# Sixteen modulation pieces moved into the filter loop, a re-staged Hyena loop, and a first token tile read partly from SBUF

## The chip, the cores and the metric

The kernel runs on one core of one Trainium2 chip. The metric is the device time of one execution in microseconds (us), as the median of several runs. Five engines work side by side: TensorE (PE in the rows; PEld is its weight load), VectorE (DVE), ScalarE (ACT), GpSimd (POOL), and SyncE (SP), which here issues nearly all DMAs. Engines wait for one another by semaphores, and each works through its own instructions in order.

## The reference

A two-layer diffusion backbone on 1024 latent tokens of width 1024, with 256 context tokens. What matters here is the first half of layer 0:

```
m  = silu(c) @ w_mod[l] + b_mod[l]              # six chunks of 1024: shift, scale, gate, twice
h  = rmsnorm(x) * (1 + scale) + shift
proj = h @ w_in                                  # 1024 x 2560: gate | RG-LRU input | Hyena (3 x 512)
y_a  = gelu(gate) * (RG-LRU forward + backward)  # 512 channels
u    = conv of 3 taps over the Hyena columns;  v, gate_0, gate_1 = split(u)
kf   = rfft of implicit filters (a small sine MLP times a decay window)
z = v
for o in (0, 1):
    z = gate_o * (irfft(rfft(z) * kf[o]) + bias * z)
x  = x + g1 * (concat(y_a, z) @ w_out)           # then expert-choice MoE; layer 1 follows
```

## The kernel before

All arithmetic is float32; the large products split each operand into a high and a low part and do three matmuls (`mm3`, L154 to L158), the split being one ACT copy and one DVE subtraction (`split`, L160 to L162). A framework turns this Python into one instruction list per engine: it ranks instructions by the order in which the program text issues them, and places each on its engine as soon as its own estimate says that operands and a buffer are free. So a later instruction of the text may run ahead of an earlier one that isn't ready, but once placed, an engine's order is fixed. Buffers with one tag rotate through a fixed count (`bufs`).

The stretches that the change touches, in order of time:

- **Modulation pieces.** `w_mod` is cut into pieces of 128 rows and 2048 columns, 1 MB each: 24 for layer 0, 16 (later 8 more) for layer 1. `ada_load` (L220) fetches one into a buffer of the pool `wr`, which has 4 buffers of 8 KB per partition; `ada_mm` (L227) multiplies it into one PSUM tile that collects 8 pieces (L235); `ada_end` (L253) closes a set of 8 with a copy, transposes and a store. `fill(n)` (L248) does one product and one load, n times. The first 8 pieces are worked off at the head of the filter loop, and the other 32 in the Hyena loop.
- **Filter loop** (`filters`, L397). Eight jobs, one for each 128 channels and each of the two orders. A job computes filter values (`signal`: products L413, windowed by DVE L414), transforms them on PE (L436 to L446), combines the results on DVE (L458 to L474) into a 1 MB tile K of the pool `wr`, and stores K to DRAM (`kd`, L475). Between the jobs, steps of the first norm run (transposes L326). PSUM has two pools: "n", 4 buffers of one bank, and "w", 2 buffers of two banks.
- **RG-LRU part**, not touched; then the **Hyena loop**. A `short(ct)` (L782) projects 128 channels (48 matmuls, L156 to L158), and applies the 3-tap conv with one ACT and two DVE instructions (L786 to L788). `tok` transposes a 128 x 1024 tile to token order on PE and copies it with ACT. A job J is one block of 128 channels at one order, and has five steps: `hy_fwd` (32 matmuls L612, and an ACT copy of half of each result, L615; it also fetches K), `hy_st1` (first butterfly, 8 DVE instructions with one operand in PSUM, L622 and L623), `hy_mid` (DVE only: an 8-point transform, the product with K, the way back; tiles raw/pq/E of tag "X", 3 buffers), `hy_inv` (16 matmuls on PE, L651) and `hy_gate` (two DVE products of the PSUM result and the gate, with stride, L659). Each of four rounds runs the job of order 0, then the job of order 1 on its result; `pend` and `drain` put a job's inverse and gate one step later.
- **Tail.** Two RG-LRU gates (`gate`, L737: projection, gelu, product with the scan's result L743, store to DRAM `ycd`), then, in an order written out by hand for PE, DVE and ACT (the `manual_schedule` block, L845 to L865), the splits of `w_out` (L986, L991), the last `drain`, a load of the first token tile's seven rows of blocks from `ycd` (`y_load`, L933), its split, and the first product of the output projection (`post_mm`). The `posts` of the other tiles follow, then the MoE.

## Time and profile before

| | us |
|---|---|
| median of 3 runs (lowest 2285.1, highest 2289.81) | 2288.9 |
| the profiled execution | 2288.93 |
| its span, from the first to the last instruction | 2287.0 |
| filter loop, from its first K to the first projection of the RG-LRU part | 31 to 128 |
| RG-LRU part | 128 to 267 |
| Hyena loop and tail, to the first matmul of the output projection | 267 to 552.4 |

Over the whole span PE is busy 93%, DVE 80%, ACT 53%. Such a share is an average over stages; the table by stretch shows where PE and DVE are both near full. A matmul's modelled time overlaps its neighbour's, so its price here is the distance from start to start.

### The profile page before, as it was taken

How to read it: one execution, taken by the hardware profiler on the slowest of the kernel's cores; microseconds unless marked ns; L12 is line 12 of the kernel's file. 1: busy time of each engine (PE TensorE's matmuls, PEld its weight loads, DVE VectorE, ACT ScalarE, POOL GpSimd, SP SyncE). 2: the span in 40 equal slices, each digit the busy share in tenths (PEclk: the TensorE clock that was granted, in tenths of full speed). 3: DMA queues.
4: the chain of work that ended last, by engine and by line, in shares of the span. 5: the costliest groups of instructions: out<-in, count | busy, mean ns of one | idle time of the engine just before them, and what ended most of it. 6: DMA issues, size and time to landing. Idle time of an engine off the chain costs nothing. (4 is left out here: it accounts for less than half of the span.)

```text
span 2287.0 us, 28692 instructions
## 1 busy us (share of the span) xinstructions
PE 2122.7 (93%) x10626; PEld 1653.2 (72%) x10626; DVE 1819.6 (80%) x2877; ACT 1201.4 (53%) x1458; POOL 126.8 (6%) x128
## 2 busy tenths in 40 slices
PE   7999998988967999999999899979679999999997
PEld 5976766756745877878778588867457777777775
DVE  5879799997596989999888534276968898888887
ACT  3658621213214777777777521134247777676774
POOL 0000000000001000000000100010010000000001
PEclk9999998989988999999999899989889999999999
DMA  7241573654848999999998744334679999999974
GB/s 283 102 138 47 194 274 122 228 195 150 293 171 313 367 395 375 391 385 377 393 377 307 233 129 154 104 119 180 254 293 365 389 367 388 370 376 379 372 268 156
DMA packets 210021, 616.09 MB, mean 269 GB/s; under 512 B 27988, under 2 KB 76758, under 8 KB 200089
## 3 DMA queue, kind: packets, MB, share of 16 engines
q1 hardware_dynamic: 198610, 572.84, 66.3%
q0 software_dynamic: 11248, 41.42, 7.1%
q8 instruction: 83, 1.36, 0.2%
q14 instruction: 56, 0.46, 0.1%
q10 hardware_dynamic: 24, 0.01, 0.0%
HBM read 558.62 MB, written 55.61 MB: 269 GB/s over the span
## 5 line engine op out<-in xcount | busy, mean ns | idle before, releaser
L162 DVE TENSOR_TENSOR e<-wx,e 128x1024 fp32r<-128x1024 f32 x516 | 617.6, 1221 | 87.0 <-ACT e L161 74.0
L161 ACT CAST e<-wx 128x1024 fp32r<-128x1024 f32 x516 | 540.2, 1051 | 226.1 <-PE P L158 224.0
L156 PE MATMUL P<-e,th 128*128 128x512 f32 x1384 | 562.9, 407 | 0.0
L158 PE MATMUL P<-e,tl 128*128 128x512 f32 x1384 | 543.5, 393 | 0.8 <-DVE tl L162 0.8
L157 PE MATMUL P<-e,th 128*128 128x512 f32 x1384 | 543.2, 392 | 0.0
L157 PEld LDWEIGHTS P<-e,th 128*128 128x128 f32 x1384 | 260.3, 188 | 60.9 <-DVE e L162 3.8
L156 PEld LDWEIGHTS P<-e,th 128*128 128x128 f32 x1384 | 260.1, 188 | 60.8 <-issue 7.2
L158 PEld LDWEIGHTS P<-e,tl 128*128 128x128 f32 x1384 | 259.9, 188 | 60.0 <-DVE tl L162 1.2
L162 DVE TENSOR_TENSOR e<-w,e 128x1024 fp32r<-128x1024 f32 x176 | 211.6, 1222 | 49.6 <-ACT e L161 29.4
L156 PE MATMUL P<-hh,wh 128*128 128x512 f32 x576 | 229.8, 400 | 16.4 <-DVE y L788 12.9
L161 ACT CAST e<-w 128x1024 fp32r<-128x1024 f32 x176 | 183.9, 1051 | 93.4 <-PE P L158 74.5
L157 PE MATMUL P<-hl,wh 128*128 128x512 f32 x576 | 229.3, 398 | 0.0
L158 PE MATMUL P<-hh,wlo 128*128 128x512 f32 x576 | 228.3, 397 | 0.1
L156 PEld LDWEIGHTS P<-hh,wh 128*128 128x128 f32 x576 | 109.5, 190 | 50.2 <-issue 24.0
L157 PEld LDWEIGHTS P<-hl,wh 128*128 128x128 f32 x576 | 109.5, 190 | 26.6 <-issue 4.3
L158 PEld LDWEIGHTS P<-hh,wlo 128*128 128x128 f32 x576 | 109.1, 189 | 26.4 <-issue 4.0
L1314 POOL DMA_INDIRECT acc<-yo,ix x31 | 50.7, 1635 | 923.9 <-DVE yo L1313 923.9
L162 DVE TENSOR_TENSOR tl<-q,th 128x512 fp32r<-128x512 f32 x128 | 84.7, 683 | 5.3 <-ACT th L161 4.1
L161 ACT CAST wh<-w 128x1024 fp32r<-128x1024 f32 x16 | 16.7, 1049 | 124.1 <-PE P L157 110.4
L1274 PE MATMUL P<-wx,xf 128*128 128x512 f32 x176 | 79.1, 592 | 0.0
L161 ACT CAST th<-q 128x512 fp32r<-128x512 f32 x128 | 71.8, 587 | 1.7 <-PE q L1239 1.7
L297 POOL TENSOR_TENSOR rs<-ms,nh 128x1 f32<-128x1 f32 x42 | 23.9, 570 | 830.2 <-issue 436.2
(411 smaller groups left out, 3022.8 us busy)
## 6 DMA issues: line engine op xcount, KB each, us to landing
wx<-i_exp_w SPq DMA_DIRECT2D x272, 1024.0 KB, 8.2
w<-i_exp_w SPq DMA_DIRECT2D x96, 1024.0 KB, 7.7
w<-i_w_mod SPq DMA_DIRECT2D x40, 1024.0 KB, 7.8
wst<-i_w_in SPq DMA_DIRECT2D x20, 512.0 KB, 4.5
kd<-w SPq DMA_DIRECT2D x8, 1024.0 KB, 5.2
w<-kd SPq DMA_DIRECT2D x8, 1024.0 KB, 8.5
acc<-res SPq DMA_DIRECT2D x16, 512.0 KB, 3.0
e<-i_exp_w SPq DMA_DIRECT2D x16, 512.0 KB, 8.0
```

The source lines that it names most:

```text
L156: t.matmul(o, lh, rh, start=start, stop=False)
L157: t.matmul(o, lh, rl, start=False, stop=False)
L158: t.matmul(o, ll, rh, start=False, stop=stop)
L161: self.nc.scalar.copy(hi, src)
L162: self.nc.vector.tensor_sub(lo, src, hi.bitcast(F32))
L297: nc.gpsimd.tensor_tensor(r, m, self.nh[:, :n], op=OP.pow)
L1274: nc.tensor.matmul(P[:, ns], f[:, k], h[:, ns], start=k == 0, stop=k == 7)
L1314: self.last = nc.gpsimd.indirect_dma_start(self.acc[l][:, :], bass.IndirectOffsetOnAxis(ap=xT[e][1][:, 0:1], axis=0), yo, None, compute_op ...
```

## The change

Three parts. In `filters`, each job but the first now does two `fill(1)` (and in jobs 1 and 2 one load more), and what is loaded is multiplied after the loop: 16 pieces that were multiplied in the Hyena loop. The Hyena loop is written anew: `hy_st1` is gone; `hy_fwd` lets ACT copy each result whole into an SBUF tile `raw`, and `hy_mid` does the first butterfly from it with two DVE instructions of 1024 columns and fetches K itself; after the inverse, ACT copies the result to SBUF (`hy_copy`), and the gate is one DVE product from SBUF; the job of order 1 now runs one round behind the job of order 0. Sixteen pieces are left in the loop: one load ahead and three `fill` in each round. Last, the first token tile takes the two blocks of the RG-LRU gates of the tail from their SBUF tiles, and the other five from `ycd` by two loads.

```diff
@@ -425,10 +425,15 @@
             if n:
                 for _ in range(3):
                     next(other, None)
+                self.fill(1)
+                if n < 3:
+                    self.ada_load()
             K = self.wr.tile([128, 8, 2, 128], F32, name="w", tag="w")
             q0 = self.ps.tile([128, 2, 2, 128], F32, name="q0", tag="n")
             qa = self.ps.tile([128, 4, 2, 128], F32, name="qa", tag="w")
             qb = self.ps.tile([128, 4, 2, 128], F32, name="qb", tag="w")
+            if n:
+                self.fill(1)
             for i in range(2):
                 mc = slice(i * 128, i * 128 + 128)
                 oc = slice(128 - i * 128, 256 - i * 128)
@@ -602,30 +607,23 @@
 
     def hy_fwd(self, p, J):
         nc = self.nc
-        J["K"] = K = self.wr.tile([128, 8, 2, 128], F32, name="w", tag="w")
-        nc.sync.dma_start(K, self.kd[J["o"]][J["qd"]])
-        J["q"] = []
+        J["raw"] = raw = p.tile([128, 8, 2, 128], F32, name="raw", tag="X", bufs=3)
         for a in range(4):
             q = self.ps.tile([128, 2, 2, 128], F32, name="q", tag="n")
             for j in range(2):
                 for ri in range(2):
                     nc.tensor.matmul(q[:, j, ri], self.G[:, a + 4 * j, ri * 128:ri * 128 + 128], J["u"][:, a + 4 * j],
                                      start=True, stop=True)
-            y4 = p.tile([128, 2, 128], F32, name="y4", tag="y4", bufs=2)
-            nc.scalar.copy(y4, q[:, 1])
-            J["q"].append((q, y4))
-
-    def hy_st1(self, p, J):
-        V = self.nc.vector
-        J["pq"] = pq = p.tile([128, 8, 2, 128], F32, name="pq", tag="X", bufs=3)
-        for a, (q, y4) in enumerate(J["q"]):
-            V.tensor_tensor(pq[:, a], q[:, 0], y4, op=OP.add)
-            V.tensor_tensor(pq[:, 4 + a], q[:, 0], y4, op=OP.subtract)
+            nc.scalar.copy(raw[:, a:a + 5:4], q)
 
     def hy_mid(self, p, J):
         V = self.nc.vector
-        pq, K = J["pq"], J["K"]
-        E = p.tile([128, 8, 2, 128], F32, name="E", tag="X", bufs=3)
+        K = self.wr.tile([128, 8, 2, 128], F32, name="w", tag="w")
+        self.nc.sync.dma_start(K, self.kd[J["o"]][J["qd"]])
+        E = J["raw"]
+        pq = p.tile([128, 8, 2, 128], F32, name="pq", tag="X", bufs=3)
+        V.tensor_tensor(pq[:, 0:4], E[:, 0:4], E[:, 4:8], op=OP.add)
+        V.tensor_tensor(pq[:, 4:8], E[:, 0:4], E[:, 4:8], op=OP.subtract)
         sub = p.tile([128, 4, 2, 128], F32, name="sub", tag="sub", bufs=1)
         self.fft8(pq, E, -1, sub)
         Z = pq
@@ -651,13 +649,15 @@
                     self.nc.tensor.matmul(q[:, j], J["Z"][:, a, ri], self.IG[:, a, ri], start=ri == 0, stop=ri == 1)
             J["r"].append(q)
 
-    def hy_gate(self, p, J):
-        dst = p.tile([128, D], F32, name="zt", tag="zt", bufs=1)
-        zv = dst.rearrange("q (p a) -> q a p", a=8)
-        gv = J["gate"].rearrange("q (p a) -> q a p", a=8)
+    def hy_copy(self, p, J):
+        J["z"] = p.tile([128, D], F32, name="zt", tag="zt", bufs=2)
+        zv = J["z"].rearrange("q (p a) -> q a p", a=8)
         for h, q in enumerate(J["r"]):
-            self.nc.vector.tensor_tensor(zv[:, h * 4:h * 4 + 4], q, gv[:, h * 4:h * 4 + 4], op=OP.mult)
-        return dst
+            self.nc.scalar.copy(zv[:, h * 4:h * 4 + 4], q)
+
+    def hy_gate(self, J):
+        self.nc.vector.tensor_tensor(J["z"], J["z"], J["gate"], op=OP.mult)
+        return J["z"]
 
     def to_tok(self, src, dst):
         nc = self.nc
@@ -707,6 +707,8 @@
                         yield from self.norm_steps(pn, rows[i], self.gg[0][0], self.mod[0], hh[i], hl[i], dve=False, hb=2)
 
                 self.filters(fk, halves())
+                while self.ada_have:
+                    self.ada_mm()
             wl = pool(sl, "wl")
             src = A["w_in"].rearrange("(k p) n -> p k n", p=128)
 
@@ -742,6 +744,7 @@
                 nc.scalar.activation(ge, P, AF.Gelu_apprx_tanh, bias=0.0, scale=1.0)
                 nc.vector.tensor_tensor(ge, ge, hs, op=OP.mult)
                 nc.sync.dma_start(self.ycd[ct * 128:(ct + 1) * 128, :], ge)
+                return ge
 
             with ExitStack() as s2:
                 pcx = pool(s2, "pcx")
@@ -789,50 +792,47 @@
                 return y
 
             def tok(y):
-                ut = py.tile([128, 8, 128], F32, name="ut", tag="u", bufs=2)
+                ut = py.tile([128, 8, 128], F32, name="ut", tag="u", bufs=1)
                 self.to_tok(y, ut)
                 return ut
 
-            pend = []
-
-            def drain():
-                J = pend.pop(0)
+            def inverse(J):
                 self.hy_inv(py, J)
-                z = self.hy_gate(py, J)
-                if J["o"] == 0:
-                    return tok(z)
-                i = J["qd"]
-                if i == 3:
-                    return z
-                nc.sync.dma_start(self.ycd[512 + i * 128:512 + (i + 1) * 128, :], z)
-
+                self.hy_copy(py, J)
+
+            J0 = dict(o=0, qd=0, u=tok(short(0)))
+            with tc.issue_after(getattr(gload, "ins", gload)):
+                nc.sync.dma_start(self.IG, A["IG"])
+                self.ada_load()
+            self.hy_fwd(py, J0)
+            J1 = None
             for i in range(4):
-                J0 = dict(o=0, qd=i, u=tok(short(i)))
-                if i == 0:
-                    with tc.issue_after(getattr(gload, "ins", gload)):
-                        nc.sync.dma_start(self.IG, A["IG"])
-                        self.fill(4)
-                else:
-                    self.fill(4)
-                self.hy_fwd(py, J0)
-                self.hy_st1(py, J0)
-                if pend:
-                    drain()
                 self.hy_mid(py, J0)
+                if J1:
+                    J1["gate"] = short(7 + i)
                 J0["gate"] = short(4 + i)
-                self.fill(4)
-                g1 = short(8 + i)
-                pend.append(J0)
-                J1 = dict(o=1, qd=i, u=drain(), gate=g1)
+                inverse(J0)
+                nxt = None
+                if i < 3:
+                    nxt = dict(o=0, qd=i + 1, u=tok(short(i + 1)))
+                    self.hy_fwd(py, nxt)
+                if J1:
+                    self.hy_mid(py, J1)
+                self.fill(3)
+                u1 = tok(self.hy_gate(J0))
+                if J1:
+                    inverse(J1)
+                    q = J1["qd"]
+                    nc.sync.dma_start(self.ycd[512 + q * 128:512 + (q + 1) * 128, :], self.hy_gate(J1))
+                J1 = dict(o=1, qd=i, u=u1)
                 self.hy_fwd(py, J1)
-                self.hy_st1(py, J1)
-                self.hy_mid(py, J1)
-                pend.append(J1)
+                J0 = nxt
+            self.hy_mid(py, J1)
+            J1["gate"] = short(11)
+            ges = [gate(py, ct, "cv", D) for ct in (2, 3)]
             for _ in range(len(self.ada_todo) + len(self.ada_have)):
                 self.fill()
             self.ada_todo = [(1, 2, k) for k in range(8)]
-            for ct in (2, 3):
-                gate(py, ct, "cv", D)
             sl.close()
             self.route_open(0, st)
             po = pool(so, "po0")
@@ -844,7 +844,10 @@
             self.mix_vecs(pb, pb)
             with tc.tile_pool(name="pq0", bufs=1, reuse_waits="tile") as pq, \
                     tc.manual_schedule(engines={mybir.EngineType.PE, mybir.EngineType.DVE, mybir.EngineType.Activation}):
-                y = self.y_load(pq, 0, 1)
+                y = pq.tile([128, 7, 128], F32, name="yc")
+                yv = self.ycd.rearrange("(k p) t -> p k t", p=128)[:, :, 0:128]
+                for a, b in ((0, 2), (4, 7)):
+                    nc.sync.dma_start(y[:, a:b], yv[:, a:b])
                 th = pq.tile([128, 7, 128], F32R, name="th")
                 tl = pq.tile([128, 7, 128], F32R, name="tl")
                 for q in range(2):
@@ -853,8 +856,10 @@
                 self.mix_cast(0)
                 self.bcast(self.sh2b, 0, 1)
                 self.wide_hi(po, ws[2])
-                z = drain()
-                self.split(th, tl, y)
+                inverse(J1)
+                z = self.hy_gate(J1)
+                for a, b, part in ((0, 2, y[:, 0:2]), (2, 3, ges[0][:, None, :128]), (3, 4, ges[1][:, None, :128]), (4, 7, y[:, 4:7])):
+                    self.split(th[:, a:b], tl[:, a:b], part)
                 self.split(self.zh, self.zl, z)
                 self.wide_lo(po, ws[2], 2)
                 self.wide_hi(po, ws[3])
```

## Rows read from the trace of the kernel before

**Rows 1.** Table by stretch: us, busy us (instructions) of each engine, clock, DMA.

```profile
31.00:128.00 97.00, 89.17 (x756) 83.99 (x754) 82.16 (x209) 53.19 (x83) 4.75 (x8) 0.98 0.43 147
128.00:134.10 6.10, 6.10 (x14) 4.46 (x15) 5.37 (x10) 2.30 (x4) 0.55 (x1) 0.50 1.01 336
267.00:552.40 285.40, 250.96 (x1438) 187.02 (x1436) 257.23 (x448) 57.24 (x85) 0.00 (x0) 0.94 0.58 213
345.00:377.00 32.00, 20.83 (x115) 14.64 (x114) 29.68 (x48) 2.63 (x3) 0.00 (x0) 0.79 0.48 162
```

**Rows 2.** Waits, 267 to 552: engine and line, releaser, us in total, times, longest.

```profile
DVE pq L622 <- ACT y L615: 17.7, 7, 6.6
PE P L156 <- DVE y L788: 12.9, 4, 4.0
DVE zt L659 <- PE q L651: 3.9, 4, 1.3
ACT th L161 <- DMA yc<-ycd: 7.5, 1, 7.5
```

**Rows 3.** Timeline: start, us, engine, line, instruction [idle before]; pieces, filter loop's end.

```profile
39.42 3.19 PE L235 MATMUL q<-w,sp 128*32 128x512 f32 x28
...
121.20 0.46 PE L445 MATMUL qb<-sd,G 128*128 128x128 f32 x2 [1.93 <-DVE kT L469]
...
128.00 0.76 PE L156 MATMUL P<-hh,wh 128*128 128x512 f32 x1 [3.29 <-DVE kT L469]
```

**Rows 4.** Who waited for the pool's tile w, filter loop (us, times); then its store.

```profile
  DVE w L464: 1.0, 1
DMA to landing us min/median/max: 3.8/5.1/5.5
```

**Rows 5.** Timeline of DVE: a product, and first-butterfly and gate instructions, with their distances.

```profile
292.61 1.22 DVE L634 TENSOR_TENSOR sub<-E,w 128x1024 f32<-128x1024 f32 x1
293.75 1.22 DVE L636 TENSOR_TENSOR pq<-E,w 128x1024 f32<-128x1024 f32 x1
...
311.45 2.19 DVE L659 TENSOR_TENSOR zt<-q,y 128x512 f32<-128x512 f32 x2
...
316.28 0.42 DVE L622 TENSOR_TENSOR pq<-q,y 128x256 f32<-128x256 f32 x1 [1.45 <-ACT y L615]
316.62 0.41 DVE L623 TENSOR_TENSOR pq<-q,y 128x256 f32<-128x256 f32 x1
```

**Rows 6.** Groups by line and form, 267 to 552: xcount, busy us, mean ns.

```profile
L659 DVE TENSOR_TENSOR zt<-q,y 128x512 f32<-128x512 f32 x16 | 17.4, 1114 | 3.9 <-PE q L651 3.9
L622 DVE TENSOR_TENSOR pq<-q,y 128x256 f32<-128x256 f32 x32 | 13.4, 420 | 18.8 <-ACT y L615 17.7
L788 DVE SCALAR_TENSOR_TENSOR y<-P,vec,y 128x1023 f32<-128x1023 f32 x12 | 15.4, 1281 | 0.1
L669 ACT COPY ut<-q 128x512 f32<-128x512 f32 x16 | 9.0, 590 | 51.7 <-PE q L668 51.7
```

**Rows 7.** Timeline of PE: one inverse after its last input.

```profile
308.76 2.94 PE L651 MATMUL q<-IG,pq 128*128 128x128 f32 x24
311.46 0.47 PE L156 MATMUL P<-hh,wh 128*128 128x512 f32 x1
```

**Rows 8.** Timeline of the tail, by engine.

```profile
538.37 5.49 ACT L986 CAST oh<-w 128x2048 fp32r<-128x2048 f32 x3
539.93 0.41 DVE L601 SCALAR_TENSOR_TENSOR pq<-sub,E 128x256 f32<-128x256 f32 x1
540.39 4.96 PE L651 MATMUL q<-IG,pq 128*128 128x128 f32 x28 [2.54 <-DVE pq L601]
545.80 2.03 DVE L659 TENSOR_TENSOR zt<-q,y 128x512 f32<-128x512 f32 x2
551.37 0.94 ACT L161 CAST th<-yc 128x896 fp32r<-128x896 f32 x1 [7.51 <-DMA yc<-ycd]
552.36 0.79 PE L156 MATMUL P<-oh,th 128*128 128x512 f32 x1 [7.00 <-ACT th L161]
```

## The prediction, made before the changed kernel ran

> **What bounds the kernel now.** I read the table by stretch first. In the filter loop (31 to 128 us) PE is busy 89.2 of 97 us and DVE 82.2; in the Hyena loop with its tail (267 to 552.4) PE is busy 251.0 and DVE 257.2 of 285.4 [rows 1]. So neither stretch has an engine to spare: in the first PE is the tighter one, in the second DVE, with PE close behind, and ACT is far from full in both (53 of 97, 57 of 285). Then the waits of the second stretch [rows 2]: DVE waits 17.7 us in 7 pieces for ACT's copies behind `hy_fwd`, of which the longest, 6.6, is the start of the loop, and 3.9 us in 4 pieces for the inverse; ACT waits 7.5 us once for the load `yc`. These are the places where one job's chain (inverse, gate, transpose, `hy_fwd`, copy) has to go round before DVE gets its next work. PE's 12.9 us of waits for L788 are the other face of it: its PSUM results stand until DVE finds time. Last I read the timeline at the ends of both stretches.
>
> **Part 1, sixteen pieces into the filter loop.** A piece is 8 matmul records; 28 of them take 3.19 us, so a piece costs 0.91 us [rows 3], and sixteen 14.6 us. Two sets also close there (`ada_end`: six transposes each and two small copies), by the same records' pace about 0.8 us each on PE. Together about 16 us of PE come into a stretch that has 97 − 89.2 = 7.8 us of PE idle. What can take them up: two gaps at its end, 1.93 and 3.29 us, where PE waits for DVE's combination of the last two jobs [rows 3], since with more PE work DVE is no longer behind; and the clock. From 128.0 to 134.1 TensorE's granted clock is 0.50, 1.2 instead of 2.4 GHz, and 14 matmuls take 6.1 us [rows 1]; it fell just after those gaps, and at full clock they would take half, so 3 us come back if the pieces fill the gaps. By the Trainium skill (TensorE: Matmul & The Clock Gate, What's actually happening) it is activity that releases the throttle; the row agrees in that idling came before the fall, and that rule speaks for this part. So at best 5.2 + 3 + about 4 of the other idle and slow time = 12 of the 16 are absorbed: cost 4 us. At worst nothing is, 16 us, and two buffers make it more. The piece's accumulator takes one of the four PSUM banks "n", which the window products and norm transposes share, and up to three pieces wait in the four buffers of `wr`, so that a job's K is left one. The trace shows this wait once: L464, the first write of K, stands 1.0 us for such a tile [rows 4]. K's buffer comes free when its store has landed, 5.1 us after its issue [rows 4]; what is queued behind a late L464 is all of DVE's later work of the job, and behind that PE's next L445. At 1 us for each of eight jobs that is 8 more: 24 us. On SP the loads stand in one queue with the stores of K, which wait for DVE; a load is 1 MB and late only if its piece is due before, and the DMA engines are 43% busy here [rows 1]. I take 10.5, nearer to the full price than to the absorbed one, since the gaps stand at the end of the loop while the pieces start in its first half.
>
> **Part 2, the Hyena loop.** The work of PE there falls by the same 16 us. The work of DVE falls too. The first butterfly is 64 instructions in all at 0.34 us from start to start, 21.8 us; after it is 16 of 1024 columns at 1.14, 18.2 us [rows 5]: 3.6 less. The gate is 16 instructions at about 1.05 us (two are merged as 2.19 in the row, less the overlap), 16.8; after it is 8 of 1024 columns from SBUF at 1.14, 9.1 [rows 5, 6]: 7.7 less. In sum 11 us, and as DVE is the tighter engine, they count. ACT takes over copies of 128x512 at 0.59 [rows 6], the pair behind the inverse with stride, which no row shows for ACT; DVE's strided 512 columns cost 1.11 [rows 6], so a copy is between 0.59 and 1.11, I take 0.8, and with 32 + 16 copies ACT stays under 100 of 285 us. That hides on ACT save at the tail, below.
>
> Against this part speaks a rule of the Trainium skill (VectorE: DVE Perf Modes, Rules for kernel authors): a matmul's result is worth copying to SBUF first only if many operations follow; the gate is one. The row says otherwise: the strided product with PSUM costs 1.11 us per 512 columns, while a whole product of 1024 from SBUF costs 1.14 in distance [rows 5, 6]. By the rule the gate would gain nothing on DVE, and the 11 would be 3.6; the row decides.
>
> Then the waits. Before, 17.7 − 6.6 (the start) − 1.4 (its second half) + 3.9 = 13.6 us of DVE idle lie within the loop [rows 2]. With order 1 a round behind, DVE always has another job's `hy_mid` ready while the chain of the first goes round, so these go. What is late next: the tag "X" has 3 buffers, and `raw` now holds one from `hy_fwd` on, so the first instruction of a `hy_mid` needs the buffer that the last job's inverse is still reading. That inverse has 24 records left after its last input, 2.7 us [rows 7]; before, DVE had the first butterfly and two more instructions to do meanwhile. Seven such changes at 2.7 are 19 us at most; the DVE work of the twelve `short`, 24 instructions of 1.28 us [rows 6], can fill them where PE has a result waiting, as it often has (12.9 us of waits [rows 2]). I take half, 9 us: 4.6 less than before, between 13.6 less and 5.4 more. K is now fetched by `hy_mid`; it is first needed some 8 us into it (two additions and the sixteen instructions of `fft8`), SP may issue it earlier, and so I cost it at nothing; where its buffer comes late, a job waits for up to a whole landing, 5.1 us by the store's row [rows 4], and I keep that for the range.
>
> **Part 3 and the tail.** From the last input of the inverse (539.93 + 0.41) to the first matmul of the output projection at 552.36 it is 12.0 us: inverse 4.96 at a falling clock, gate 2.03, then ACT's split of `yc`, which waits for the load, and that for the store of the last gate tile [rows 2, 8]. After, two blocks come from SBUF, and the others were stored a round earlier; in ACT's written order the split stands behind the two copies of the inverse. So inverse 3 to 5, one copy 0.8, a split of 256 columns 0.4, some waits: 6 us, a gain of 6. Its bound is PE: the splits of `w_out` (5.49 us [rows 8]) start when the last projection has released its memory, and one more `short` (ct 11) and four pieces stand in the tail, so the last projection may end later than DVE's last `hy_mid`; then the gain is 0. The three further splits of the first tile are small and lie under PE's products.
>
> **The sum.** Filter loop +10.5; Hyena −11 − 4.6; tail −6. That is −11 against the profiled execution, 2288.93 us, which is the median of the runs as well. PE would then have 251 − 16 = 235 us of work in 264, 89%, and DVE 246, 93%; since before they stood at 88 and 90 I give back 2 us for pieces that don't fit: **2280 us**. The RG-LRU part, the posts and the MoE behind keep their lengths, for their loads are issued relative to the same work.
>
> **The rivals.**
> 1. The filter loop pays more than the Hyena loop gets: K waits for a `wr` buffer in each job, as L464 did once [rows 4], and PE behind it. Filter +24, Hyena −14 with the tail: 2299. It decides once the wait is over 1 us in most jobs. For it: PE and DVE are both full there, and the sign of three pieces held. Against it: DMA has room, and a longer job gives the store more time.
> 2. PE's work only moves: the pieces cost their full 16, and the loop gives 16: 2289, no change. For it: in both stretches PE is near full, and PE's total is the same.
> 3. The skew doesn't do what it says: the three buffers of "X" make DVE wait for each inverse, 19 us, and the tail is bound by PE. Filter +10.5, Hyena −11 + 5.4: 2294.
> 4. The gaps and the slow clock of the filter loop are filled (+4), and DVE runs without a gap in the Hyena loop (−11 − 13.6 − 6): 2262.
>
> **Chances.** Forecast 0.50, rivals 1 to 4 0.14, 0.17, 0.09, 0.10. The measurement tells 0.2%, 4.6 us, from no change. The forecast's own range, 2271 to 2288, lies below 2284.3 but for a tenth of its chance; rival 4 is faster; rival 2 is mostly "same", rivals 1 and 3 slower: faster 0.57, same 0.22, slower 0.21. For 8 in 10 the range takes in most of rivals 1 and 4: 2264 to 2299.
>
> **What would show it.** Right: the stretch up to the first projection of the RG-LRU part some 10 us longer, with PE near full and no half clock behind it; in the Hyena stretch no L622 or L623, DVE busy about 246 us, its waits for ACT's copies gone but for the start, and short waits for the inverse in their place; the first matmul of the output projection without a wait for a load. Wrong: waits of L464 or L413 for buffers in the filter loop; DVE idle over 20 us in the Hyena loop; a PE that runs the tail's projections after DVE's last `hy_mid`; or stages behind that do not just shift.

## The result, and the profile after

The changed kernel takes 2309.7 us (median of 4 runs, 2308.75 to 2311.13) beside 2288.4 for the kernel before on the same chip: ratio 1.0088, 95% interval 1.0076 to 1.0100. That is 20 us slower, where 2280 was forecast, and above the range's end of 2299.

Where it went, by the profiled executions (the span after is 2307.2 us). Line numbers after the filter part have moved: L622 to L625, L659 stays the gate, L787 and L788 are L790 and L791, L651 is L649. The table by stretch, columns as in [rows 1]: filter loop to the first projection (the time before is 31 to 128); first conv to the first matmul of the output projection, whole; then its three parts: start, first butterfly to the end of the last `hy_mid`, tail.

```profile
31.00:147.00 116.00, 110.33 (x890) 86.91 (x888) 86.19 (x215) 53.99 (x85) 4.81 (x8) 0.99 0.74 270
282.80:574.30 291.50, 240.96 (x1333) 192.42 (x1331) 245.25 (x388) 77.36 (x97) 0.00 (x0) 0.91 0.42 149
...
282.80:296.50 13.70, 13.70 (x81) 11.88 (x80) 3.69 (x4) 3.40 (x6) 0.00 (x0) 1.00 0.98 368
296.50:568.20 271.70, 222.50 (x1227) 175.97 (x1225) 241.36 (x383) 71.56 (x88) 0.00 (x0) 0.90 0.40 142
568.20:574.30 6.10, 4.76 (x28) 4.57 (x28) 0.20 (x1) 2.39 (x4) 0.00 (x0) 0.76 0.00 0
```

The same three parts in the trace of before:

```profile
267.00:280.80 13.80, 11.72 (x65) 8.82 (x64) 7.23 (x7) 3.49 (x5) 0.00 (x0) 1.00 0.95 378
280.80:540.30 259.50, 234.23 (x1346) 173.38 (x1344) 242.40 (x436) 49.16 (x78) 0.00 (x0) 0.95 0.56 203
540.30:552.40 12.10, 5.01 (x29) 4.82 (x29) 7.60 (x7) 4.59 (x4) 0.00 (x0) 0.78 0.70 225
```

The filter loop is 116 us instead of 97, with PE busy 21.2 us longer. The RG-LRU part is 3 us shorter, for a reason that no run takes apart, so the Hyena part begins 16 us later than before, and it takes 291.5 us instead of 285.4 [rows 1]: 6 longer, where 19.6 less were forecast (21.6, less the 2 given back). Within it, the start is as it was and the tail has fallen by 6.0. DVE's work has fallen from 257.2 to 245.3. But the middle has grown by 12.2, although DVE has only 1.0 us less to do there: its idle time rose from 259.5 − 242.4 = 17.1 to 271.7 − 241.4 = 30.3 us. The stages behind shift, and are within 2 us of their length before (1732.9 us against 1734.6).

The waits of that stretch (engine and line, releaser, us in total, times, longest), to be laid beside [rows 2]:

```profile
PE q L649 <- DVE pq L591: 32.3, 4, 25.0
DVE y L790 <- ACT y L789: 17.3, 4, 11.2
DVE zt L659 <- ACT zt L656: 16.2, 5, 6.0
DVE pq L625 <- ACT raw L617: 10.0, 1, 10.0
PE P L156 <- DVE y L791: 7.2, 2, 3.7
```

Three things stand out. First, DVE's waits for the copies behind `hy_fwd` are gone except at the loop's start: before, 17.7 − 6.6 = 11.1 us of them lay inside. Second, in their place stand 17.3 us for the conv's operand, that is for a projection on PE, where before had 0.3; and 16.2 for the copies of the inverse, of which 6.0 is the tail. Third, PE, which makes DVE wait early, itself waits 25 us in one piece at the end.

### The profile page after: what moved, and what is told of

Read it like the earlier page. It is cut to its first block, busy times and chain, and to the rows that moved or that the text cites. A ratio compares the mean times of both kernels' runs of the same rounds, so it can differ in the third digit from the quotient of the medians.

```text
span 2307.2 us, 28640 instructions
## 1 busy us (share of the span) xinstructions
PE 2124.6 (92%) x10626; PEld 1655.5 (72%) x10626; DVE 1811.1 (78%) x2824; ACT 1225.4 (53%) x1477; POOL 126.7 (5%) x128
## 5 line engine op out<-in xcount | busy, mean ns | idle before, releaser
L156 PEld LDWEIGHTS P<-hh,wh 128*128 128x128 f32 x576 | 109.0, 189 | 39.8 <-issue 12.2
L157 PEld LDWEIGHTS P<-hl,wh 128*128 128x128 f32 x576 | 109.3, 190 | 24.6 <-issue 1.8
```

What stands on the lines that cost most here:

```text
L156: t.matmul(o, lh, rh, start=start, stop=False)
L157: t.matmul(o, lh, rl, start=False, stop=False)
```

## The experiments

Differences are the measured ratio less 1, times 2289 us, with its interval, against the kernel before on the same chip. "Loop" is the stretch from the first conv to the first matmul of the output projection in the run's trace; it is 285.4 us before and 291.5 after. A trace is one execution; those of e9, e10 and e11 took 4.4, 3.4 and 10.1 us more than their run's median, in part by a slower clock in the filter loop (last section). Code is cut to the lines that matter: e1, e3 to e6, e8 and e11 edit the kernel before, the others the changed kernel.

| run | us | against before | loop |
|---|---|---|---|
| e1_pieces | 2306.2 | +15.8 (12.1 to 19.7) | 284.5 |
| e2_loop_tail | 2296.2 | +6.9 (4.1 to 9.4) | 294.8 |
| e3_bodies | 2302.0 | +11.9 (8.0 to 15.8) | 300.6 |
| e4_tail | 2284.0 | −5.3 (−7.6 to −3.2) | 279.1 |
| e5_fwd | 2296.8 | +7.8 (4.6 to 11.2) | 292.5 |
| e6_gate | 2296.2 | +5.5 (3.0 to 7.8) | 293.4 |
| e7_skew_oldfwd | 2289.1 | +0.2 (−2.5 to 3.0) | 286.0 |
| e8_tail_gate1 | 2282.2 | −8.0 (−10.3 to −6.0) | 279.7 |
| e9_round0 | 2299.7 | +10.8 (6.9 to 14.4) | 279.9 |
| e10_chain | 2299.2 | +10.1 (6.2 to 14.0) | 280.0 |
| e11_filt14 | 2297.5 | +9.6 (6.2 to 13.0) | – |
| e12_skew_old | 2289.2 | +1.1 (−1.6 to 4.1) | 286.0 |
| e13_skewold_late | 2279.1 | −12.4 (−16.5 to −8.0) | 276.6 |
| e14_oldfwd_late | 2277.5 | −12.4 (−16.9 to −8.0) | 277.6 |
| e15_new_late | 2281.9 | −7.1 (−10.5 to −3.7) | 279.7 |

### Which part costs

**e1_pieces**: the kernel before with part 1 alone.

```diff
+                self.fill(1)
+                if n < 3:
+                    self.ada_load()
...
+            if n:
+                self.fill(1)
...
-                    self.fill(4)
+                    self.fill(2)
```

> The kernel before with part 1 alone: the filter loop takes sixteen modulation pieces as in the changed kernel, and the Hyena loop, otherwise as before, does two fills at each of its places instead of four. Theory A (in the changed kernel the pieces cost their full PE price in the filter loop, and DVE's wait for the loop's end and a slow clock come on top): the first projection after the filter loop starts 17 to 20 us later than before, the Hyena loop gives back at most 8 of it because DVE is its tighter engine; the whole 10 to 17 us slower than before. Rival (PE's work only moves, the Hyena loop gives back what the filter loop pays): within 4 us of before.

Measured +15.8, within theory A and nearly the 16 us of PE that the prediction had counted for the pieces. Its loop, with 16 pieces less, is 284.5 us beside 285.4:

```profile
284.40:568.90 284.50, 239.69 (x1334) 192.04 (x1332) 256.53 (x445) 55.74 (x81) 0.00 (x0) 0.91 0.44 156
```

PE has 11.3 us less to do there than in [rows 1], DVE 0.7 less, and the stretch is 0.9 shorter. So what PE gives up in this loop is not returned: DVE, with 256.5 us of work and its waits, sets its length.

**e2_loop_tail**: the change without part 1; 32 pieces as `fill(8)` in each round.

```diff
-                self.fill(3)
+                self.fill(8)
```

> The changed kernel without part 1: no pieces in the filter loop, and all 32 in the new Hyena loop (eight fills in each round instead of three). Theory A (the new order of the loop is at fault: PE runs projections ahead and is full in the middle, DVE waits for them, and the last job stands alone at the end): filter loop as before, loop and tail 6 us longer than before or more, up to 14 since PE gets 16 us more in the stretch where it is full; the whole 4 to 14 us slower than before. Rival (the loop is good and suffers only from what the moved pieces shift): 10 to 20 us faster than before.

Measured +6.9, within theory A: parts 2 and 3 lose by themselves. (The lines of part 1 go too; they are not shown.) DVE's waits hold one of 18.2 us for a projection, in the first round; e13 to e15 come back to it.

**e3_bodies**: the old order of jobs, with the new forward step and the new gate step.

```diff
-            nc.scalar.copy(y4, q[:, 1])
+            nc.scalar.copy(raw[:, a:a + 5:4], q)
...
-            V.tensor_tensor(pq[:, a], q[:, 0], y4, op=OP.add)
-            V.tensor_tensor(pq[:, 4 + a], q[:, 0], y4, op=OP.subtract)
+        V.tensor_tensor(pq[:, 0:4], E[:, 0:4], E[:, 4:8], op=OP.add)
+        V.tensor_tensor(pq[:, 4:8], E[:, 0:4], E[:, 4:8], op=OP.subtract)
...
-            V.tensor_tensor(zv[:, h * 4:h * 4 + 4], q, gv[:, h * 4:h * 4 + 4], op=OP.mult)
+            self.nc.scalar.copy(zv[:, h * 4:h * 4 + 4], q)
+        V.tensor_tensor(dst, dst, J["gate"], op=OP.mult)
```

> The kernel before with only the new bodies of the steps: whole copies by ACT behind the forward transform, first butterfly by two DVE instructions from SBUF, the inverse copied by ACT and gated by one DVE product; the order of the loop, the pieces and the tail's loads as before. Theory A (the bodies are good, the order is at fault): DVE's busy time in the loop falls by 11 us and the loop by 6 to 12; the whole 6 to 12 us faster. Rival (the copies lie on the chain that goes round for each job, eight times some 2 us, so that DVE waits for ACT what it saves): within 4 us of before.

Measured +11.9; both expectations miss. What is seen is the rival's mechanism, but dearer than it had it: DVE's work did fall, to 246.8 us, and its waits rose by more:

```profile
DVE pq L620 <- ACT raw L614: 30.6, 5, 10.4
DVE zt L657 <- ACT zt L656: 12.4, 8, 4.1
```

Before, these two places held 17.7 and 3.9 us [rows 2].

**e4_tail**: part 3 alone (two rows from SBUF, two loads for the others, split part by part).

```diff
-                y = self.y_load(pq, 0, 1)
+                for a, b in ((0, 2), (4, 7)):
+                    nc.sync.dma_start(y[:, a:b], yv[:, a:b])
```

> The kernel before with part 3 alone: two blocks of the first token tile from SBUF, the other five by two loads. Theory A: the first matmul of the output projection starts 3 to 5 us earlier after the last inverse, since ACT no longer waits for the load behind the last store; the whole 3 to 5 us faster. Rival (the splits of w_out on ACT and DVE, which stand ahead, are the next to be late): under 2 us.

Measured −5.3, just past the 3 to 5 of theory A. Parts 1, 2 and 3 can now be read: +16, +12 (e2 less e4) and −5 are 23, beside +20 measured for all.

### Which body costs

**e5_fwd** takes the forward step of e3 alone, **e6_gate** the gate step alone.

> The kernel before with the new forward step alone: ACT copies each of the four results whole into one SBUF tile, and the first butterfly is two DVE products over 1024 columns that need all four copies. Gate, order of the jobs, pieces and tail as before. Theory A (the whole-tile butterfly lengthens the chain: it can't start on the first quarter while PE is at the second): DVE waits on the copies rise from 17.7 us to about 28, its work falls by 3 to 4 us, and the kernel is 5 to 10 us slower than before, more than half of the 12.7 of both bodies. Rival B (the strided copies behind the inverse are the cost): within 3 us of before.

> The kernel before with the new gate step alone: ACT copies the inverse's two results with stride to SBUF, about 1.0 us each, and one DVE product of 1024 columns follows. All else as before. Theory A: the chain gains two copies one behind the other, but DVE saves about 7 us of work; 1 to 5 us slower than before. Rival B (these copies are what cost in the bodies): 8 to 12 us slower. Rival C (the saved DVE work counts): 3 to 7 us faster.

Measured +7.8 and +5.5, together 13.3 beside 11.9 for both; the forward step is with its theory A, the gate step stands just above its expected 1 to 5. Waits of e5, then of e6:

```profile
DVE pq L620 <- ACT raw L614: 26.8, 5, 10.6
DVE zt L657 <- PE q L649: 3.6, 3, 2.3
```

```profile
DVE pq L622 <- ACT y L615: 24.6, 10, 7.0
DVE zt L659 <- ACT zt L658: 14.9, 8, 3.8
```

In e5 the butterfly can't begin before all four copies are done; before, it began on the first quarter while PE was at the second. In e6 two copies stand between the inverse and the gate, 1.1 us each (row L656 of the change, in the last section), and the forward step behind them comes late too (24.6 against 17.7).

**e8_tail_gate1**: e4, with the new gate step only for order-1 jobs, whose result goes to DRAM.

```diff
+            if J["o"] and J["qd"] < 3:
+                self.nc.scalar.copy(zv[:, h * 4:h * 4 + 4], q)
```

> The kernel before with the change of the tail (2284 us), and with the ACT copy and the product from SBUF only for the order-1 jobs of the first three blocks, whose result goes to DRAM and which nobody waits for; the order-0 jobs keep the product from PSUM. Theory A (DVE is the tighter engine of the loop and the copy costs only where a chain stands behind it): 1 to 4 us below 2284, so 2280 to 2283. Rival B (any work taken from DVE ends as waiting, since the chain sets the pace): within 1 us of 2284 or above.

Measured −8.0, so 2.7 below e4; the two intervals overlap only at their ends (−7.6 to −3.2 and −10.3 to −6.0). The direction fits theory A, that the DVE work which the copy saves counts where no chain stands behind it; the size is not clear of the noise.

### What the order of the jobs costs, and why

**e7_skew_oldfwd**: e2 with the old forward step. **e12_skew_old**: with the old gate step as well, its two products right behind the inverse.

```diff
-            nc.scalar.copy(raw[:, a:a + 5:4], q)
+            nc.scalar.copy(y4, q[:, 1])
+            J["q"].append((q, y4))
...
+            V.tensor_tensor(pq[:, a], q[:, 0], y4, op=OP.add)
+            V.tensor_tensor(pq[:, 4 + a], q[:, 0], y4, op=OP.subtract)
```

> The changed kernel's Hyena loop and tail (order 1 a round behind, ACT copy of the inverse, product from SBUF, two rows of the first tile from SBUF), with all 32 pieces in the Hyena loop and with the old forward step: half of each result copied by ACT, eight butterfly instructions from PSUM right behind the matmuls. It stands against the same with the new forward step, 2296 us, and against before with the tail alone, 2284. Theory A (the whole-tile forward step is what eats the skew's gain): 2278 to 2287, so 9 to 18 below its twin. Rival B (the skewed order itself makes DVE wait, whatever the step): 2292 to 2300.

> The skewed order and the changed tail with both old bodies: half copies and eight butterfly instructions from PSUM, and two products from PSUM right behind the inverse; 32 pieces in the Hyena loop. Theory A (the skew itself is worth nothing here; all that the Hyena part loses is the bodies' longer chain): 2282 to 2287, as with the tail alone (2284). Rival B (the skew does take away DVE's waits, and the new bodies hid that): 2270 to 2279.

Measured +0.2 and +1.1: e7 lies between its two theories, e12 above both of its own. With old bodies the skewed order is 6.4 slower than the old order with the same tail (e4). The trace of e12 has it in one place (start, us, engine, line, instruction, idle before and releaser):

```profile
330.24 1.28 DVE L788 SCALAR_TENSOR_TENSOR y<-P,vec,y 128x1023 f32<-128x1023 f32 x1 [12.71 <-ACT y L787]
```

DVE stands 12.7 us for a projection. On PE, eight pieces, of which seven are shown, run in front of and between its matmuls:

```profile
311.98 3.64 PE L235 MATMUL q<-w,sp 128*32 128x512 f32 x32
318.06 1.07 PE L235 MATMUL q<-w,sp 128*32 128x512 f32 x8
321.59 1.06 PE L235 MATMUL q<-w,sp 128*32 128x512 f32 x8
325.12 1.06 PE L235 MATMUL q<-w,sp 128*32 128x512 f32 x8
```

**e13_skewold_late**, **e14_oldfwd_late**, **e15_new_late**: e12, e7 and e2 with the 32 pieces handed out otherwise.

```diff
-                self.fill(8)
+                self.fill((2, 8, 10, 11)[i])
```

> The skewed order with both old bodies and the changed tail (2289 us), with the 32 pieces of the Hyena loop handed out as 2, 8, 10 and 11 to the four rounds instead of 8 to each. There DVE waited 12.7 us at one place in the first round for a projection that stood behind pieces on PE, while PE idled 20 us at the loop's end. Theory A (where the pieces stand is what the skew loses by): the wait at that place falls below 4 us, 2276 to 2282. Rival B (PE's work before that place is too long without pieces as well, or the wait moves to the second round): 2285 to 2290.

> The same handing out of pieces, in the skewed order with the old forward step and the new gate step (2289 us as it was, with a wait of 12.8 us at the same place). Theory A: 2276 to 2282, and the new gate step no dearer than the old one. Rival B: 2285 to 2290.

> The same handing out of pieces in the changed Hyena loop and tail with both new bodies and no piece in the filter loop (2296 us as it was, with a wait of 18.2 us at the same place). Theory A: the 18 us fall to about 8, 2284 to 2290, so that the new forward step still costs 6 or more against the run beside it. Rival B (the new forward step only cost because pieces stood in the way): within 2 us of the run beside it.

Measured −12.4, −12.4 and −7.1, in each case with theory A (e15 even 2 below its range), against +1.1, +0.2 and +6.9 with eight pieces a round: 12.6 to 14.0 us for where 32 pieces stand. In e13 the wait at that place is gone, and DVE's longest wait for a conv is 3.1 us:

```profile
DVE y L788 <- ACT y L787: 3.1, 1, 3.1
```

So the skewed order with late pieces is 7.1 us faster than the old order with the same tail (e13 less e4), and with eight pieces a round 6.4 slower. No run has the old order with late pieces; in e4 DVE waits only 0.3 us for a conv, so the wait that late pieces take away isn't there. The new gate step costs nothing that can be seen in the skewed order (e14 and e13). With the new forward step it is 5.3 slower (e15 less e14, whose intervals overlap by 2.5), but that is not shown to be the step's own price: in e15 DVE's two splits of `w_out` stand between the instructions of the last `hy_mid`, for which the last inverse waits, and in e14 behind it, under the inverse. By the starts, one split puts off the next instruction by 2.2 us (525.53 less 523.33), so the two by some 4.4, an estimate. First e15, then e14, whose last `hy_mid` ends at 536.24:

```profile
523.33 2.28 DVE L989 TENSOR_TENSOR ol<-w,oh 128x2048 fp32r<-128x2048 f32 x1
525.53 1.22 DVE L630 TENSOR_TENSOR sub<-raw,w 128x1024 f32<-128x1024 f32 x1
526.66 2.28 DVE L989 TENSOR_TENSOR ol<-w,oh 128x2048 fp32r<-128x2048 f32 x1
```

```profile
536.16 4.49 DVE L994 TENSOR_TENSOR ol<-w,oh 128x2048 fp32r<-128x2048 f32 x2
```

e14 and e13 are the fastest versions found, 12 us below before and some 32 below the change.

**e9_round0** and **e10_chain** ask the same of the change itself, with its 16 pieces in the filter loop. e9 puts the first round's pieces where PE stood idle; e10 puts the next job of order 1 ahead of the next block's projection.

```diff
-                self.ada_load()
+                for _ in range(3):
+                    self.ada_load()
...
                 J0["gate"] = short(4 + i)
+                if i == 0:
+                    self.fill(3)
                 inverse(J0)
```

```diff
                 inverse(J0)
+                if J1:
+                    self.hy_mid(py, J1)
+                u1 = tok(self.hy_gate(J0))
                 nxt = None
...
-                if J1:
-                    self.hy_mid(py, J1)
                 self.fill(3)
-                u1 = tok(self.hy_gate(J0))
```

> The changed kernel, with the first round's three pieces loaded ahead and multiplied before the first inverse, where PE stood idle for 9.7 us and then ran at half clock for 13.7; the number of pieces in the loop is the same. Theory A (what PE loses there makes its projections late, and DVE waits 11.2 us for one at 368 us): the half clock of 312 to 325 shrinks, the wait falls below 5 us, and the time is 4 to 9 below the changed kernel: 2301 to 2306. Rival B (DVE's wait comes from the order of PE's work, not from its lost time): the wait stays near 11, and the time within 2 us of 2310.

> The changed kernel, with the gate, transposes and hence the next order-1 job written ahead of the next block's projection and forward step (and two buffers for the transposed tile, which this order needs). Theory B of the run beside it (the order of PE's work: a whole projection of 11 us stands between the inverse and the next job that DVE could have): the wait of 11.2 us goes, 2299 to 2305. Theory A (PE's lost time makes it late in any order): the wait moves to the other job's forward step, 2307 to 2312.

Measured 9.3 and 10.0 below the change (by the ratios), so each met the theory that it was made for (e9 a little past its 4 to 9). Either edit takes the 11.2 us wait away; which of the two causes made it in the change is not shown. In the change, PE waits and is then slow (table by stretch, after):

```profile
308.20:320.20 12.00, 2.39 (x4) 1.01 (x4) 12.00 (x14) 2.13 (x2) 0.00 (x0) 0.65 0.26 87
311.70:325.30 13.60, 7.44 (x26) 5.78 (x27) 13.60 (x24) 1.17 (x2) 0.00 (x0) 0.50 0.23 77
367.70:378.90 11.20, 11.20 (x56) 7.91 (x55) 0.02 (x1) 2.15 (x2) 0.00 (x0) 1.00 0.62 184
```

At 308 PE idles for PSUM tiles that DVE releases late, the granted clock falls to 0.50 for 13.6 us, and at 368 PE is busy throughout while DVE does nothing. In e9, whose loop begins 5.5 us later, the same part of the round is full, at full clock, and the wait for the conv is 2.9 us in all:

```profile
314.00:318.00 4.00, 4.00 (x19) 3.33 (x18) 4.00 (x4) 0.62 (x1) 0.00 (x0) 1.00 0.69 266
318.00:330.00 12.00, 12.00 (x60) 9.75 (x58) 11.84 (x19) 2.32 (x3) 0.00 (x0) 1.00 0.58 179
```

```profile
DVE y L790 <- ACT y L789: 2.9, 2, 1.8
```

But e9 changed PE's order as well as its idle time: between the first `hy_fwd` and the first inverse, 102 matmuls of projections are recorded in e9, and 58 in the change (table by stretch for the projections' tile alone, after, then e9):

```profile
295.50:320.20 24.70, 14.90 (x58) 11.08 (x58) 5.14 (x4) 2.41 (x2) 0.83 0.46 175
301.00:328.10 27.10, 24.17 (x102) 18.84 (x102) 5.12 (x4) 2.41 (x2) 1.00 0.79 288
```

In e10 the conv's wait is 3.1, but some of it has moved to the copies behind `hy_fwd`, 17.0 us instead of 10.0. e10 also has a second buffer for the transposed tile; what that is worth alone is not tested.

### The end of the filter loop

**e11_filt14**: e1 with no piece left behind the last job (shown against e1).

```diff
-                self.fill(1)
+                if n < 7:
+                    self.fill(1)
+                else:
+                    self.ada_mm()
...
-            if n:
-                self.fill(1)
+            if n == 7:
+                self.ada_mm()
+            elif n:
+                self.fill(1)
```

> The pieces alone (2306 us), with 14 instead of 16 in the filter loop: the last job multiplies its two pieces and loads none, so none is left to be multiplied behind the loop; the other two go back to the Hyena loop. Theory A (a good part of the 17 us is at the loop's end: two pieces and the wait for the last load behind the last job, 2.8 us, and the half clock after it, 3.4 us): 8 to 12 us slower than before, 2297 to 2301. Rival B (the pieces cost their PE time wherever they stand): 14/16 of 17, 15 us slower than before, 2302 to 2306.

Measured +9.6 (6.2 to 13.0) instead of +15.8 (12.1 to 19.7), with theory A: two pieces less save some 6 us, more than the 2 that their share of the price is, though the intervals overlap by 0.9. The profiled execution took 2307.6 us, 10 above the run's median, so its trace is not used for the size; in it PE has no wait for a load and no half clock behind the loop, as expected. How much of the 6 is the wait, the clock and the pieces is left open.

## Why the prediction was wrong, step by step

**Part 1: mis-sized.** Forecast +10.5, measured +15.8 alone (e1), 15.9 at the first conv in the trace after. In the filter loop PE's busy time rose by 21.2 us where 16 were counted, and its idle time fell only from 7.8 to 5.7. A piece was priced at 0.91 us from a block of 28 records [rows 3]. Among other matmuls it costs more:

```profile
L235 PE MATMUL q<-w,sp 128*32 128x512 f32 x160 | 25.0, 622 | 2.8 <-DMA w<-i_w_mod 2.8
```

That is 20 pieces (4 of before and 16) in 25.0 us, 1.25 each: a piece alone spans 1.06 us, some are cut in two by other matmuls, and one ran at the half clock. Next, the cover: the two gaps of 1.93 and 3.29 us did go, but the pieces left over for the loop's end brought a new one of 2.77 for a load, and the half clock behind it stayed:

```profile
144.33 1.89 PE L235 MATMUL q<-w,sp 128*32 128x512 f32 x8 [2.77 <-DMA w<-i_w_mod]
147.05 0.80 PE L156 MATMUL P<-hh,wh 128*128 128x512 f32 x1 [0.83 <-ACT wh L161]
```

**"The work of PE there falls by the same 16 us"**: PE's busy time fell by less, 10.0 us (250.96 to 240.96; 11.3 in e1), and almost nothing of it came back as time, 0.9 us in e1. This was not in the sum as a gain, so it cost nothing there; it makes part 1 a loss by itself.

**DVE's work in the Hyena loop: right.** Forecast −11, measured −12.0, of which 1.0 is the last gate, which now lies just past the stretch's end (574.10). The gate is 8 instructions of 1225 ns after, where 16 of 1114 stood [rows 6], the butterfly 16 of 1221.

**That this work counts in full, and that DVE's waits go: wrong, the failing step.** The sum had DVE's 11 us of saved work "count" because DVE is the tighter engine, and its waits in the loop fall by 4.6. Between the first butterfly and the end of the last `hy_mid`, DVE's work fell by 1.0 us instead, and its idle time rose by 13.2.

First, the work. At the loop's start DVE did 7.2 us of work before and does 3.7 after; in the tail it is 7.6 and 0.2. Apart from the last gate, some 9 us of that were not saved but moved into the middle: a conv and a weight split from the start, the RG-LRU gate's product L743 and the two splits of `w_out`, L991, from the tail. Where they were, they stood beside waits that DVE had anyway; in the middle they take the place of the saved work, 241.4 us against 242.4. The splits show it best. Before, and in e4, they run behind the last `hy_mid`, while PE is at the last inverse; in the change they stand between the instructions of the last `hy_mid`, for which that inverse waits. In order: before, whose last `hy_mid` ends at 540.34 [rows 8]; e4, where it ends at 540.0; the change, where it ends at 568.14:

```profile
541.40 4.48 DVE L991 TENSOR_TENSOR ol<-w,oh 128x2048 fp32r<-128x2048 f32 x2
```

```profile
541.06 4.48 DVE L995 TENSOR_TENSOR ol<-w,oh 128x2048 fp32r<-128x2048 f32 x2
```

```profile
548.41 2.30 DVE L996 TENSOR_TENSOR ol<-w,oh 128x2048 fp32r<-128x2048 f32 x1
555.15 2.30 DVE L996 TENSOR_TENSOR ol<-w,oh 128x2048 fp32r<-128x2048 f32 x1
```

The shorter tail doesn't need this: e4 has it, with the splits where they were, and keeps its 5.3 us. It is the new order that puts them there; what that costs in the change is not separated by a run.

Second, the waits. The bodies lengthen the chain that a job goes round. I costed the copies by ACT's load ("hides on ACT"), not by what stands behind them; e5 and e6 price this at 7.8 and 5.5 us in the old order. What the new order does to the waits comes next.

**The waits: half right.** Those behind `hy_fwd` inside the loop did go, 11.1 us. But the forecast for what is late next, the "X" buffer still read by the inverse, 9 us, was wrong: L625 waits only at the start in the change. Such waits show in e9 (4.8 us in 3) and e15 (5.3 in 1). Late instead were the projections, 17.3 us, and the copies of the inverse, 10.2 inside the loop, where 3.9 stood for the inverse itself. I had looked at PE's load over the whole loop, 89%, and not over time: in the skewed order PE is the tighter engine for the first three quarters, where DVE has 24 of its 30.3 us of idle time in the middle, and idle for more than half of the end:

```profile
296.50:400.00 103.50, 93.75 (x506) 74.93 (x505) 82.42 (x126) 28.51 (x37) 0.00 (x0) 0.93 0.38 135
400.00:500.00 100.00, 100.00 (x564) 81.26 (x563) 96.99 (x152) 26.03 (x33) 0.00 (x0) 1.00 0.41 140
500.00:574.30 74.30, 33.50 (x187) 24.35 (x185) 62.15 (x108) 19.42 (x22) 0.00 (x0) 0.72 0.40 142
```

The "2 us given back for pieces that don't fit" were for this. Where the pieces stand, with what follows from it, is worth 13 to 14 us with 32 pieces (e12 to e15), and 9 with the change's own 16 (e9). Of the signs that the prediction named for being wrong, DVE idle over 20 us in the loop is the one that came.

**Part 3 and the tail: right.** Forecast 6 us from the last input of the inverse to the first matmul of the output projection; it is 568.14 to 574.34, 6.2, and there is no wait for a load:

```profile
568.20 4.76 PE L649 MATMUL q<-IG,pq 128*128 128x128 f32 x28 [3.08 <-DVE pq L606]
573.00 1.07 ACT L656 COPY zt<-q 128x512 f32<-128x512 f32 x1 [0.74 <-PE q L649]
573.86 0.42 ACT L161 CAST th<-yc 128x256 fp32r<-128x256 f32 x1
574.34 0.50 PE L156 MATMUL P<-oh,th 128*128 128x512 f32 x1 [1.38 <-ACT th L161]
```

**The rivals.** The price of the first (filter +24) is nearest to the trace's +19, but its mechanism is not there: the first write of K waits for its tile once, 1.0 us, as before [rows 4].

```profile
  DVE w L469: 1.0, 1
```

Half of the second came true (PE's work only moves), without the return. Of the third, the buffers were no cause and the tail wasn't bound by PE; DVE's added idle, 13.2 us, is more than twice its 5.4. No rival had a PE that is late early on and idle at the end, though the waits of PE for L788 [rows 2] showed already that two PSUM tiles tie the two engines together.

**The rule set aside.** The Trainium skill (VectorE: DVE Perf Modes, Rules for kernel authors) would copy a matmul's result to SBUF first only for many operations. I let the row decide, and on DVE's time the row was right (8 × 1.23 = 9.8 us instead of 17.4). On the kernel's time, in the old order, the rule's advice would have been the better (e6, +5.5), for a reason of which neither speaks: the copy stands in a chain. Where nobody waits behind it (e8), or where the skewed order has other work (e14), no cost of the copy shows.

## What to carry to other kernels

Work taken off the tighter engine counts only where that engine isn't then waiting: price a split or copy by what stands behind it in the job's chain, not by the load of the engine that takes it. When a loop is re-staged, look at both engines' load by stretches of the new order, and put movable work (here the modulation pieces) where the other engine sets the pace; here 13 us hung on that and what followed from it. Work that stands beside a wait is free only there: see where a new order puts it (here some 9 us of DVE work from both ends of the loop) before counting what else was saved.

## What the runs showed of the hardware that was not expected

A piece of 8 column-tiled matmuls costs 0.91 us in a long block of its kind and spans about 1.06 alone between other matmuls, 1.89 at the half clock. ACT's copy of a 128x512 result from PSUM costs 1.11 us when it is written with stride 8, and 0.59 without:

```profile
L617 ACT COPY raw<-q 128x512 f32<-128x512 f32 x32 | 18.7, 594 | 20.0 <-PE q L615 14.7 <-DVE pq L606 5.0
L656 ACT COPY zt<-q 128x512 f32<-128x512 f32 x16 | 17.3, 1110 | 55.7 <-PE q L649 55.7
```

I had taken 0.8; 1.11 is the upper bound that the prediction gave, and the same as DVE's strided product [rows 6].

In the change, TensorE's granted clock was at the lower of its two levels, 1.2 GHz, from 311.7 to 325.3 us, after PE had idled 3.7 us and during further short gaps; in e9, where PE has no gap in that part of the round, it stayed at 2.4. This agrees with the Trainium skill (TensorE: Matmul & The Clock Gate, What's actually happening), by which activity releases the throttle. As e9 changed PE's order there too, it isn't shown that the three pieces alone would have kept the clock. Nor is the slow stretch peculiar to the change; the kernel before has one as long, which begins in the second of PE's waits of 2.7 and 4.0 us for L788:

```profile
362.80:376.50 13.70, 7.05 (x28) 6.06 (x29) 12.47 (x22) 0.00 (x0) 0.00 (x0) 0.50 0.24 88
```

The same code can also get either clock. The filter loop of e9 is that of the change, and in both traces PE waits 0.8 us for DVE at 62 to 64 us; behind that wait the clock was at 1.2 GHz for 10 us in e9, and stayed at 2.4 in the change (after, then e9):

```profile
61.00:71.00 10.00, 8.81 (x61) 5.48 (x60) 8.88 (x22) 3.28 (x5) 0.00 (x0) 1.00 0.76 292
61.00:71.00 10.00, 9.21 (x45) 5.27 (x44) 9.05 (x22) 2.20 (x4) 0.00 (x0) 0.67 0.74 283
```

The traces of e10 and e11 show the same fall. By these rows it costs some 5 us (an estimate: half of 10 us), more than the 3 us that the forecast of part 1 gave the clock; how often it comes is not shown.
